# Four edits to a one-core transformer-layer kernel: modulation sums by transposes, chunk states in seven pieces, four output tiles in token halves, last output in four transfers from two queues

## The chip, the cores and the metric

The kernel runs on one core of a Trainium2 chip. A core has a matrix engine (TensorE, PE in the profile; its weight loads are shown apart as PEld), three further compute engines (VectorE or DVE, ScalarE or ACT, GpSimd or POOL), a queue engine that issues transfers (SyncE, SP), and 16 transfer engines (DMA). Each engine runs its own instructions in order and waits on semaphores for the others. Operands lie in an on-chip memory of 128 partitions; TensorE writes its sums into banks of a second memory, from which the other engines read them. The metric is the device time of one execution in microseconds (us); of several runs the median is given.

## What is computed

One layer of a diffusion backbone over 512 latent tokens of width 1024, with 256 context tokens. In outline:

```python
def reference(x, c, ctx, c_ctx, w_mod, b_mod, ...):
    mod = silu(c) @ w_mod + b_mod                       # six vectors of 1024
    sh1, sc1, gt1, sh2, sc2, gt2 = split(mod, 6)
    h_lat = rmsnorm(x, norm1_g) * (1 + sc1) + sh1       # the same for ctx with c_ctx
    p = h @ w_in                                        # z, xs/B/C, dt, q, k, v, gates
    y_ssd = ssd_bidir(...)                              # state-space mixer, 4 groups, both directions
    y_att = window_ctx_attention(...)                   # 16 heads, window of 128, context keys, sink
    o = (g_ssd * (y_ssd @ w_o_ssd) + g_att * (y_att @ w_o_att)) @ w_out
    x = x + gt1 * o
    x = x + gt2 * conv_ffn(rmsnorm(x, norm2_g) * (1 + sc2) + sh2, w_up, ..., w_down)
    return rmsnorm(x, final_g)
```

`ssd_bidir` cuts the 512 tokens into four chunks of 128. For each chunk a state (decayed sum of B times the scaled inputs) is carried on from the chunk before; the states of the backward direction go the other way round. The first states come from the context tokens.

## The kernel before

Activations are held with channels on the partitions and tokens along the free axis, 512 columns (`L`). Every fp32 product is split into a high and a low part: for a weight block of 128x128, TensorE does three matmuls, high weight by high input (line 192), high by low (line 193), low by high (line 195). A `gemm` makes an output tile of 128 channels over eight such blocks, so it has 24 matmuls of 512 columns for the latent tokens (`LAT`) or of 256 for the context (`CTX`).

**Weights.** A tile's weights arrive by `load_raw` as 512 KB in one of three raw buffers (`wraw`), issued on SyncE's queue. ScalarE makes the high part (line 149), VectorE the low part (line 150), each into one of two buffers, and then the raw buffer is free again. `run` walks a list of steps and loads the weights of the next step ahead of the one that runs. The 32 blocks of the modulation weights (`wm`, `msteps`) go through the same raw buffers, without a split. `weave(a, b)` puts the steps of b evenly between those of a.

**Modulation sums (`m_step`).** The four vectors that are needed late (gt1, sh2, sc2, gt2; 32 columns of 128 in `mod2`) come from 32 blocks, four blocks to a group of four columns, so eight groups. VectorE multiplies each block by the conditioning vector and adds up over the blocks in one tile `tm` (lines 550 and 552). With a group's last block, TensorE sums over the partitions by four fp32 matmuls of the tile's four 128-column pieces by a column of ones (line 556), each done in two passes, and VectorE adds the bias to the 128x4 result (line 558).

**Projection and chunk states.** For each of four groups, six projection steps follow each other (B, C, four tiles of xs). Each ends with a convolution over tokens and a silu (lines 860 to 869, the last being `tc` at line 869). The result must be transposed to tokens on the partitions: it is put on a list `TURN`, and `turn()` (lines 883 to 890) does the transposes of all that is on the list, four of 128x128 for the latent tokens and two for the context (line 888). After the four xs tiles, `states()` puts six pieces on a list `BETWEEN`; `gemm` takes one piece after every block k with k % 3 == 1, that is three in a gemm of eight blocks. The pieces are `first` (the outstanding transposes, then VectorE weighs the context's inputs for the backward direction, `xw`, line 947), `second` (TensorE sums the context, line 978, and VectorE weighs for the forward direction), `third` (the same sum for the forward direction, and the first latent chunk is weighed), and three times `back` (TensorE sums a chunk, line 960; GpSimd decays the state before, line 962; VectorE adds, line 963; the next chunk is weighed). The gemms they go into are those of the next group's B step (`b_fn`: one for the latent, one for the context tokens), and for the last group those of steps that fill in (branch gates and z).

**Output tiles.** After the merge of the branches, `out_step(o)` makes tiles 0 to 4 of the product with `w_out` over all 512 tokens: gemm, VectorE adds to x (line 1238), ScalarE squares (line 1187) and VectorE adds up the squares. These five are woven with six modulation blocks (numbers 18 to 23): one each after tiles 0 to 3, two after tile 4. Blocks 16 to 19 make a group, and so do 20 to 23. Tiles 5 to 7 are in `out_last`: token half by token half, three tiles a half, 24 matmuls of 256 columns each (lines 1196 to 1198), written down in TensorE's order by hand. Their weights go to buffers of their own (`wlast`, in space that the SSD output held before), loaded and split like the rest. In the second half's gemms stand the steps of the second norm for the first half: `half_sums`, `root`, `spread`.

**Tail (`down_last`, `finish`).** The last tile of the down projection is made in token halves, and with each half the final norm is done: squares, sums, root (on GpSimd, line 245), spread over the partitions by transposes, then eight chunks of 128x256 are scaled (VectorE line 1383; for the second half GpSimd does two of them, chunks 5 and 6, line 1381, from copies that ScalarE has scaled before) and sent out by five transfers, all on SyncE's queue (line 1385): chunks (0, 1), (2, 3), (4), (5, 6), (7).

The order of instructions on each engine is found by a scheduler from estimates, except where the program writes it out (`manual_schedule`); a list of instructions in the built program shows what order it chose. In that order the changed program differs from the one before around the output tiles, as told under the change.

## Time and profile before

| what | value |
|---|---|
| median of 3 runs | 1293.3 us (1292.84 to 1293.32) |
| profiled execution | 1291.25 us |
| span of the profile | 1289.5 us |
| mean granted TensorE clock | 0.998 |
| ScalarE busy | 664.8 us (52%) |
| GpSimd busy | 138.6 us (11%) |
| moved by transfers | 168.66 MB, mean 131 GB/s |

The profile is of one execution. The span goes from its first instruction to its last; the device time is some 2 us more. The chain of waits follows back from the last instruction to what released it, so a share of it is a share of the time that can be saved at all. A group's line reads: source line, engine, operation, tile written from tiles read, shape, count, then busy us and mean ns of one, and last the idle time of the engine just ahead of them with what ended it. A row of the timeline has start, duration, engine, line, operation, and in square brackets the idle time ahead of it. Matmuls are pipelined, so a matmul's own 390 ns is not what it adds; the distance from one start to the next is.

### The profile page before, as it was taken

The numbers are of one execution on the slowest core, as the hardware profiler recorded it, in microseconds if no ns is written. First come the engines' busy times: TensorE is split into PE (matmuls) and PEld (weight loads), VectorE is DVE, ScalarE is ACT, GpSimd is POOL, SyncE is SP. The second block draws the span as 40 slices with busy tenths as digits, with TensorE's granted clock in tenths as the row PEclk, the third lists the DMA queues.
The fourth block names the chain that finished last, engine by engine and source line by source line (L and its number), as shares of the span: only waits on it lengthen the run. The fifth ranks groups of instructions, "written<-read, shape, count | busy, mean of one in ns | idle before, by whom it ended". The sixth has DMA issues, their size and how long they took to land.

```text
span 1289.5 us, 17298 instructions
## 1 busy us (share of the span) xinstructions
PE 1260.1 (98%) x6482; PEld 1025.6 (80%) x6482; DVE 899.2 (70%) x1431; ACT 664.8 (52%) x1230; POOL 138.6 (11%) x113
## 2 busy tenths in 40 slices
PE   7999999999999999999999999999999999999997
PEld 4698777887778878788787777888888888888886
DVE  3867888778495588888888757776677767772323
ACT  3568888767434466475673744223544444442221
POOL 0000000000000043433434440000200000000000
PEclk9999999999999999999999999999999999999999
DMA  8621112222345245454445558867133433333331
GB/s 321 255 94 51 42 58 66 66 74 66 99 127 184 82 117 137 139 134 131 137 140 170 165 192 290 252 221 229 33 115 115 131 114 114 115 107 93 92 101 66
DMA packets 86931, 168.66 MB, mean 131 GB/s; under 512 B 6784, under 2 KB 42112, under 8 KB 86848
## 3 DMA queue, kind: packets, MB, share of 16 engines
q1 hardware_dynamic: 86848, 167.56, 41.5%
q8 instruction: 51, 0.84, 0.3%
q14 instruction: 32, 0.26, 0.1%
HBM read 150.62 MB, written 16.91 MB: 130 GB/s over the span
## 4 chain that ended last, share of the span: by engine, by line
PE 84%; DVE 7%; ACT 5%; issue 2%; DMA 1%; POOL 0%; SPq 0%; DVEq 0%; ACTq 0%; POOLq 0%
PE acc L193 21%; PE acc L192 21%; PE acc L195 21%; PE mis L1054 2%; PE mis L1047 2%; PE score L668 2%; PE pt L697 2%; PE mis L404 2%; PE mis L960 1%; PE po L702 1%; DVE wlo L150 1%; PE mis L888 1%; PE mis L978 1%; PE po L703 1%; PE acc L1196 1%
## 5 line engine op out<-in xcount | busy, mean ns | idle before, releaser
L150 DVE TENSOR_TENSOR wlo<-wraw,whi 128x1024 fp32r<-128x1024 f32 x161 | 203.8, 1266 | 133.0 <-ACT whi L149 131.7
L149 ACT CAST whi<-wraw 128x1024 fp32r<-128x1024 f32 x161 | 166.7, 1036 | 220.7 <-PE acc L193 186.6
L192 PE MATMUL acc<-hlh,whi 128*128 128x512 f32 (+1 forms) x496 | 204.1, 412 | 0.1
L193 PE MATMUL acc<-hll,whi 128*128 128x512 f32 (+1 forms) x496 | 196.1, 395 | 0.0
L195 PE MATMUL acc<-hlh,wlo 128*128 128x512 f32 (+1 forms) x496 | 195.4, 394 | 0.2 <-DVE wlo L150 0.2
L192 PE MATMUL acc<-mh,whi 128*128 128x512 f32 x376 | 146.5, 390 | 0.0
L193 PE MATMUL acc<-ml,whi 128*128 128x512 f32 x376 | 146.4, 389 | 0.0
L195 PE MATMUL acc<-mh,wlo 128*128 128x512 f32 x376 | 146.3, 389 | 0.0
L192 PEld LDWEIGHTS acc<-hlh,whi 128*128 128x128 f32 (+1 forms) x496 | 93.0, 187 | 21.3 <-issue 4.1
L193 PEld LDWEIGHTS acc<-hll,whi 128*128 128x128 f32 (+1 forms) x496 | 93.0, 187 | 19.9 <-issue 4.1
L195 PEld LDWEIGHTS acc<-hlh,wlo 128*128 128x128 f32 (+1 forms) x496 | 92.8, 187 | 19.5 <-issue 1.0
L195 PEld LDWEIGHTS acc<-mh,wlo 128*128 128x128 f32 x376 | 70.6, 188 | 14.8
L192 PEld LDWEIGHTS acc<-mh,whi 128*128 128x128 f32 x376 | 70.6, 188 | 14.7
L193 PEld LDWEIGHTS acc<-ml,whi 128*128 128x128 f32 x376 | 70.6, 188 | 14.6 <-DVE ml L1165 0.2
L962 POOL TENSOR_TENSOR st<-st,eT 128x512 f32<-128x512 f32 x24 | 32.8, 1368 | 410.3 <-ACT st L980 396.7
L860 ACT ACTIVATE ta<-acc,half 128x512 f32<-128x512 f32 (+1 forms) x66 | 46.6, 706 | 41.0 <-PE acc L195 41.0
L245 POOL TENSOR_TENSOR rs<-ms,phalf 128x2 f32<-128x2 f32 (+1 forms) x7 | 6.1, 877 | 548.9 <-DVE ms L244 548.9
L675 DVE CUSTOM_DVE_ANT_0 p<-score,winm,nsink 128x512 f32<-128x512 f32 (+1 forms) x64 | 52.0, 812 | 15.0 <-PE score L668 14.2
L192 PE MATMUL acc<-fh,whi 128*128 128x512 f32 x154 | 60.0, 390 | 0.0
L195 PE MATMUL acc<-fh,wlo 128*128 128x512 f32 x154 | 59.9, 389 | 0.0
L193 PE MATMUL acc<-fl,whi 128*128 128x512 f32 x154 | 59.9, 389 | 0.0
L679 ACT ACTIVATE p<-p,mneg 128x512 f32<-128x512 f32 (+1 forms) x64 | 49.7, 777 | 17.2 <-DVE mneg L675 16.9
(320 smaller groups left out, 2818.8 us busy)
## 6 DMA issues: line engine op xcount, KB each, us to landing
wraw<-wup SPq DMA_DIRECT2D x44, 512.0 KB, 3.6
fb<-cs_d SPq DMA_DIRECT2D x32, 512.0 KB, 6.7
wraw<-wm SPq DMA_DIRECT2D x32, 512.0 KB, 3.6
wraw<-wx SPq DMA_DIRECT2D x24, 512.0 KB, 3.6
wm<-wm SPq DMA_DIRECT2D x16, 512.0 KB, 8.1
wraw<-wz SPq DMA_DIRECT2D x16, 512.0 KB, 3.6
wraw<-wos SPq DMA_DIRECT2D x16, 512.0 KB, 4.6
wraw<-wdn SPq DMA_DIRECT2D x16, 512.0 KB, 3.5
```

Of the source, the lines that this page charges most:

```text
L149: S.copy(hi[:, :n], r[:, :n])
L150: V.tensor_tensor(lo[:, :n], r[:, :n], raw(hi[:, :n]), ALU.subtract)
L192: T.matmul(ps, wh, xh[:, k0 + k, :], start=a, stop=False)
L193: T.matmul(ps, wh, xl[:, k0 + k, :], start=False, stop=False)
L195: T.matmul(ps, wl, xh[:, k0 + k, :], start=False, stop=b)
L404: T.matmul(pg[i], w[a][:, i * P : (i + 1) * P], h[b], start=st and a + b == 0, stop=en and a == 1, skip_group_check=True,)
L668: T.matmul(ps[:, o : o + w], Q[h][:, b * P : (b + 1) * P], k[:, j, z[0] * P : z[0] * P + w], start=v == 0 and o % 512 in (0, P), stop=v == ...
L675: V.tensor_tensor_reduce(p[:, :n], ps[:, o0 : o0 + n], m, op0=ALU.add, op1=ALU.min, scale=1.0, scalar=nsink[:, h : h + 1], accum_out=mn,)
L679: S.activation(p[:, :n], p[:, :n], AF.Exp, bias=mn, scale=-1.0, accum_out=den[:, i : i + 1])
L697: T.transpose(pt[:, i * P : (i + 1) * P], pts[i][:, c * P : (c + 1) * P], ident)
L860: S.activation(o[:, :n], ps[:, :n], AF.Identity, scale=hcol(base_w, stride + i), bias=hcol(base_b, i))
L962: G.tensor_tensor(h8(n), h8(s), bc64(eT[:, z0 : z0 + 8, c]), ALU.mult)
```

## The change

- The four matmuls by ones become four transposes into one bank, and VectorE sums each 128-column piece with one reduction and adds the bias in a second small instruction.
- `turn(n)` does the first n transposes on the list and leaves the rest. A piece that does only the first entry (the latent tokens' four transposes) stands ahead of `first`, which makes seven pieces; the last `back` then falls into the gemm after.
- Output tile 4 moves from `out_step` to `out_last`, which now has four tiles in two halves. The six modulation blocks are woven with four tiles: one after tile 0, two after tile 1, one after tile 2, two after tile 3. On SyncE's queue the loads before ran: tile 0, m18, tile 1, m19, tile 2, m20, tile 3, m21, tile 4, m22, m23, tiles 5 to 7. They now run: tile 0, m18, tile 1, m19, m20, tile 2, m21, tile 3, m22, m23, tiles 4 to 7. On VectorE the first product of m20 stands ahead of the split of tile 3, its second one behind it.
- The output of each half goes in four transfers of two chunks, alternately from SyncE's and ScalarE's queue; the chunks that GpSimd scales are 4 and 5.

```diff
--- before.py
+++ after.py
@@ -553,9 +553,10 @@
             if kk == 3:
                 ps = misb()
                 for c in range(4):
-                    T.matmul(ps[:, c : c + 1], acc[:, c * P : (c + 1) * P], ones[:, 0:1], start=True, stop=True)
+                    T.transpose(ps[:, c * P : (c + 1) * P], acc[:, c * P : (c + 1) * P], ident)
                 z = slice(4 * cg, 4 * cg + 4)
-                V.tensor_tensor(mod2[:, z], ps[:, 0:4], vec[:, V_BMOD + 16 + 4 * cg : V_BMOD + 20 + 4 * cg], ALU.add)
+                V.tensor_reduce(mod2[:, z], ps.rearrange("p (c q) -> p c q", c=4), axis=AX.X, op=ALU.add)
+                V.tensor_tensor(mod2[:, z], mod2[:, z], vec[:, V_BMOD + 16 + 4 * cg : V_BMOD + 20 + 4 * cg], ALU.add)
 
         return [("m", i)], fn
 
@@ -880,14 +881,14 @@
     GR = [{} for _ in range(4)]
     TURN = []
 
-    def turn():
-
-        for t, n, put in TURN:
+    def turn(n=None):
+
+        for t, n_, put in TURN[:n]:
             ps = misb()
-            for c in range(n):
+            for c in range(n_):
                 T.transpose(ps[:, c * P : (c + 1) * P], t[:, c * P : (c + 1) * P], ident)
             put(ps)
-        TURN.clear()
+        del TURN[:n]
 
     def proj_steps(g):
         d = GR[g]
@@ -986,6 +987,9 @@
             def first():
                 turn()
                 weigh_ctx(1)
+
+
+            BETWEEN.append(lambda: turn(1))
 
             def second():
                 sum_ctx(1)
@@ -1223,8 +1227,8 @@
         return fn
 
 
-    for o in (5, 6, 7):
-        ELSEWHERE["out", o] = piece_in("yh%d" % (o - 5))
+    for o in (4, 5, 6, 7):
+        ELSEWHERE["out", o] = piece_in("yh%d" % (o - 4))
 
     def out_step(o):
         def fn(w):
@@ -1241,8 +1245,8 @@
         return [("out", o)], fn
 
     def out_last(*w):
-        xt = [cp.tile([P, L], F32, tag="ld", name="ld", bufs=3) for _ in range(3)]
-        for i, o in enumerate((5, 6, 7)):
+        xt = [ldt[0]] + [cp.tile([P, L], F32, tag="ld", name="ld", bufs=3) for _ in range(3)]
+        for i, o in enumerate((4, 5, 6, 7)):
             nc.sync.dma_start(xt[i], xT[o // 2, :, (o % 2) * L : (o % 2 + 1) * L])
         pf = F["pf"] = misb()
         F["r2"] = []
@@ -1255,17 +1259,17 @@
 
         with tc.manual_schedule(engines={mybir.EngineType.PE}):
             for u, z in enumerate(HALF):
-                for i in range(3):
+                for i in range(4):
                     after = {}
                     if u == 1:
                         after = {0: {5: root}, 1: {4: spread}}.get(i, {})
-                    if i == 2:
+                    if i == 3:
                         after[2] = lambda u=u: half_sums(pf, q2, u)
                     ps = accb()
                     half_gemm(ps, mh, ml, z, w[i], 8, 0, 8, after)
-                    x = x1[1][:, 1 + i, z]
-                    V.scalar_tensor_tensor(x, ps[:, :HL], g1h[:, 5 + i : 6 + i], xt[i][:, z], ALU.mult, ALU.add)
-                    if i == 0:
+                    x = x1[1][:, i, z]
+                    V.scalar_tensor_tensor(x, ps[:, :HL], g1h[:, 4 + i : 5 + i], xt[i][:, z], ALU.mult, ALU.add)
+                    if i < 2:
                         sq = half_squares([x])[0]
                         V.tensor_tensor(q2[:, z], q2[:, z], sq, ALU.add)
                 F["sq2"] = half_squares([x1[1][:, 2 + i, z] for i in range(2)])
@@ -1374,7 +1378,7 @@
             if u:
                 r3s = tmp("tc")[:, :HL]
                 S.copy(r3s, rms_spread(r["s"], 2)[:, :HL])
-            for cs in ((0, 1), (2, 3), (4,), (5, 6), (7,)):
+            for i, cs in enumerate(((0, 1), (2, 3), (4, 5), (6, 7))):
                 for c in cs:
                     x = x1[c // 4][:, c % 4, z]
                     if u and c in scaled:
@@ -1382,7 +1386,7 @@
                     else:
                         V.scalar_tensor_tensor(x, x, col(V_FG, c), r3[:, :HL], ALU.mult, ALU.mult)
                 n, c = len(cs), cs[0]
-                nc.sync.dma_start(
+                (S if i % 2 else nc.sync).dma_start(
                     out[c * P : (c + n) * P, z].rearrange("(a p) t -> p a t", a=n), x1[c // 4][:, c % 4 : c % 4 + n, z]
                 )
                 if c == 2:
@@ -1400,7 +1404,7 @@
             V.scalar_tensor_tensor(xo, ps[u][:, :HL], mod2[:, 31:32], xo, ALU.mult, ALU.add)
             r["sq"] = half_squares([xo])
 
-        for i, c in enumerate((5, 6)):
+        for i, c in enumerate((4, 5)):
             scaled[c] = tmp("te")[:, :HL]
             S.activation(scaled[c], x1[1][:, c % 4, HALF[1]], AF.Copy, scale=col(V_FG, c))
         ps = [accb(), accb()]
@@ -1420,9 +1424,9 @@
         + fill[n3:]
         + [os_step(o) for o in range(2)]
         + weave([os_step(o) for o in range(2, 8)], msteps[8:18])
-        + weave([out_step(o) for o in range(5)], msteps[18:24])
+        + weave([out_step(o) for o in range(4)], msteps[18:24])
         + [([], vectors)]
-        + [([("out", o) for o in (5, 6, 7)], out_last), ([], close_c1)]
+        + [([("out", o) for o in (4, 5, 6, 7)], out_last), ([], close_c1)]
         + weave([up_step(t) for t in range(NFF)], msteps[24:])
         + [down_step(o) for o in range(7)]
         + [([("dn", 21 + i) for i in range(3)], down_last)]
```

## The prediction

> **What bounds the kernel now.** First the page's busy line and the shares of the chain that ended last.
>
> ```profile
> span 1289.5 us, 17298 instructions
> ...
> PE 1260.1 (98%) x6482; PEld 1025.6 (80%) x6482; DVE 899.2 (70%) x1431; ACT 664.8 (52%) x1230; POOL 138.6 (11%) x113
> ...
> PE 84%; DVE 7%; ACT 5%; issue 2%; DMA 1%; POOL 0%; SPq 0%; DVEq 0%; ACTq 0%; POOLq 0%
> ```
>
> TensorE is busy for 98% of the span, and 84% of the chain lies on it, so an edit pays if it takes instructions out of TensorE's stream, or shortens one of the few places where that stream waits. VectorE and ScalarE count where they are late with something TensorE wants, and in the tail, where TensorE has nothing left. So I went by stage: the chain of waits for each edited line, TensorE's own rows around the state pieces, the transfer queue's rows around the output tiles, the tail. The profiled execution took 1291.25 us with a span of 1289.5; the median shown is 1293.3, so 2 us of the forecast is only the step from that execution to the median.
>
> **A, modulation sums.** Chain of waits, first and last of the eight groups of sums, and a row of sixteen transposes:
>
> ```profile
> 522.80 1.75 PE mis L1076 x16
> ...
> 579.01 0.79 PE mis L556 x8
> ...
> 1155.75 0.79 PE mis L556 x8
> ```
>
> Groups of instructions:
>
> ```profile
> L963 DVE TENSOR_TENSOR st<-st,mis 128x512 f32<-128x512 f32 x24 | 16.3, 680 | 2.0 <-PE mis L960 2.0
> L556 PE MATMUL mis<-ones,tm 128*128 128x1 f32 x64 | 7.6, 239 | 0.0
> ```
>
> The 64 matmuls are eight groups of four columns, two passes each: 0.79 us a group on the chain. Four transposes instead cost 4 × 1.75/16 = 0.44 by the first row. The saving is 0.35 a group by these rows; where a dense matmul follows, I read about 0.1 more lost after the old group (a weight load per single-column pass), so 0.35 to 0.47, eight times: −2.8 to −3.8, and I take **−3.5 us**. VectorE gets a reduction of 128x512 from PSUM and a 128x4 add where it had one such add. No reduction stands in the trace. The nearest row reads 512 columns from PSUM and takes 0.68 us, the two-operand form, and I take 0.7; eight make 5.6 us on an engine that is idle 30% of the span. I cost that at nothing: it is hidden while TensorE runs the next gemm, whose low weights were split one step ahead. With that cover gone it costs 0.7 a group (last rival). The bank of sums is read some 0.7 us longer; four others remain.
>
> **B, chunk states in seven pieces.** TensorE's rows at the second and third group's first piece, then one row of the longest waits (total, times, longest):
>
> ```profile
> 610.80 0.39 PE L192 MATMUL acc<-hlh,whi 128*128 128x512 f32 x1
> 611.97 0.41 PE L888 MATMUL mis<-ident,tc 128*128 128x128 f32 x2 [0.78 <-DVE tc L869]
> ...
> 695.07 0.41 PE L888 MATMUL mis<-ident,tc 128*128 128x128 f32 x2 [0.78 <-DVE tc L869]
> ...
> 698.67 0.70 PE L978 MATMUL mis<-xw,Bkc 128*128 128x512 f32 x1 [0.23 <-DVE xw L947]
> ```
>
> ```profile
> PEld mis L978 <- DVE xw L947: 4.2, 8, 0.9
> ```
>
> A gemm's matmuls start 0.23 apart, so between 610.80 and 611.97 TensorE lost 1.17 − 0.23 = 0.94 us waiting for the context columns' convolved tile; the same, with the same idle entry, ahead of 695.07. The weight loads of the context sums then waited 4.2 us in all for the weighted tile, in part beside a matmul still running; the one case with a number on TensorE itself is the 0.23 of 698.67, against a longest wait of 0.9. I count half of the 4.2 as TensorE's, so all stalls here are 1.9 + 2.1 = 4 us. The change puts the four transposes of the main columns into a piece of their own, and the two of the context columns one piece later, so nine matmuls of the gemm stand between where seven stood. Two more of 0.227 hide 0.45 of each 0.94; the waits for the weighted tile may go or stay, and I take half of their 2.1. That is −0.9 and −1.1: **−2 us**, from 0 to −4. Nothing is added. What moves: the last piece of the backward states now goes into the next gemm, so in the last group its VectorE work, one weighted tile, stands later, just ahead of the chunks' first use; a loss there would be up to that tile's product, 0.7 by the row of 680 ns, and the bound of 0 covers it only with a gain elsewhere.
>
> **C, output tile 4 in halves.** First the price on TensorE, from the chain at the border:
>
> ```profile
> 890.32 0.23 PE acc L195
> 890.55 0.79 PE mis L556 x8
> ...
> 891.56 0.12 PE acc L1197
> ```
>
> A tile was 24 matmuls at 0.227; in halves it is 48 at 0.120: **+0.3 us**. The larger effect is in the order of loads. With four tiles woven with six modulation steps, two steps now follow output tile 1, so the step's second block is loaded ahead of tile 2's weights. There are three raw buffers, and each load is issued when the next buffer comes free, as issues and releases show (before). SyncE's queue, then VectorE, the list of issues (median us to landing) and ScalarE:
>
> ```profile
> 861.55 0.33 SPq L145 DMA_DIRECT2D wraw<-wout  x1
> 866.44 0.33 SPq L145 DMA_DIRECT2D wraw<-wm  x1
> 867.71 0.33 SPq L145 DMA_DIRECT2D wraw<-wout  x1
> ...
> 869.99 0.33 SPq L145 DMA_DIRECT2D wraw<-wm  x1
> ...
> 875.46 0.33 SPq L145 DMA_DIRECT2D wraw<-wout  x1
> 877.24 1.90 SPq L145 DMA_DIRECT2D wraw<-wm  x2
> ...
> 881.86 3.95 SPq L145 DMA_DIRECT2D wraw<-wout  x3
> ```
>
> ```profile
> 863.93 0.75 DVE L552 SCALAR_TENSOR_TENSOR tm<-wraw,csil,tm 128x512 f32<-128x512 f32 x1 [0.90 <-DMA wraw<-wm]
> ...
> 865.20 1.22 DVE L150 TENSOR_TENSOR wlo<-wraw,whi 128x1024 fp32r<-128x1024 f32 x1
> ...
> 868.73 1.23 DVE L150 TENSOR_TENSOR wlo<-wraw,whi 128x1024 fp32r<-128x1024 f32 x1
> ...
> 874.10 0.17 DVE L558 TENSOR_TENSOR mod<-mis,vec 128x4 f32<-128x4 f32 x1
> 874.21 1.23 DVE L150 TENSOR_TENSOR wlo<-wraw,whi 128x1024 fp32r<-128x1024 f32 x1
> ...
> 876.47 2.32 DVE L552 SCALAR_TENSOR_TENSOR tm<-wraw,csil,tm 128x512 f32<-128x512 f32 x3
> 879.71 0.75 DVE L1238 SCALAR_TENSOR_TENSOR x<-acc,g1h,te 128x512 f32<-128x512 f32 x1 [0.92 <-PE acc L195]
> 880.61 1.23 DVE L150 TENSOR_TENSOR wlo<-wraw,whi 128x1024 fp32r<-128x1024 f32 x1 [0.15 <-ACT whi L149]
> ```
>
> ```profile
> wraw<-wm SPq DMA_DIRECT2D x32, 512.0 KB, 3.6
> ```
>
> ```profile
> 886.43 1.05 ACT L149 CAST wlast<-wraw 128x1024 fp32r<-128x1024 f32 x1 [5.30 <-DMA wraw<-wout]
> 888.24 1.05 ACT L149 CAST wlast<-wraw 128x1024 fp32r<-128x1024 f32 x1 [0.23 <-DMA wraw<-wout]
> ```
>
> The issues of 866.44 and 869.99 come with the ends of the splits of 865.20 and 868.73. A load issued at 881.86 had landed at 886.43: 4.57 us with others in flight, and 1.05 for the cast and 1.23 for the low part follow. Now the changed order. Its slot at 861.55 goes to the modulation block; tile 2's weights go when tile 1's are split, 865.0 (the product of 863.93 no longer ahead of the split) to 866.4, and are split by 871 to 873. Tile 3's load goes then, and its low part ends by 877 to 879.5; TensorE wants it at 879.2 (tile 2 ended shortly ahead of 879.71; the shorter sums take off 0.35). The last two modulation blocks and tile 4's weights wait in turn for that split, for the block held since 861.55 (its second product stands behind the split on VectorE, 0.7 + 0.75) and for the next one (two products, 1.5): tile 4's load goes at 880 to 882.5, lands 4.6 later at 884.6 to 887, and its low part is ready at 887 to 889.5. TensorE has finished tile 3 at 879.2 + 24 × 0.227 = 884.6, the four transposes at 885.1, and wants that low part at 885.3: a new stall of 1.5 to 4.5 us, 0 if all lands as early as 3.6 us (the usual figure of a raw load in the list of issues). I take **+2.7 us**. Before, this margin was there: the same weights were split in step at 880.6. Behind the late split on VectorE stand only those of tiles 5 to 7, at 1.83 us of landing distance against 2.9 us of matmuls per half tile, so the stall comes once. The tail of the last output half and the norm after it are unchanged in place.
>
> **D, last output.** SyncE's issues by line, VectorE's and GpSimd's last work, and us, DMA share and GB/s in the last stretches:
>
> ```profile
> L1385 SPq DMA_DIRECT2D out<-x x10: 345/395/466, 1278.8 to 1286.6; - x10
> ```
>
> ```profile
> 1282.98 2.44 DVE L1383 SCALAR_TENSOR_TENSOR x<-x,vec,mis 128x256 f32<-128x256 f32 x6 [1.37 <-PE mis L251]
> ```
>
> ```profile
> 1283.70 1.41 POOL L1381 TENSOR_TENSOR x<-te,tc 128x256 f32<-128x256 f32 x2 [1.25 <-ACT tc L1376]
> ```
>
> ```profile
> 1286.00:1287.00 1.00, 0.00 (x0) 0.00 (x0) 0.00 (x0) 0.00 (x0) 0.00 (x0) 0.50 1.02 358
> 1287.00:1288.00 1.00, 0.00 (x0) 0.00 (x0) 0.00 (x0) 0.00 (x0) 0.00 (x0) 0.50 1.09 381
> 1288.00:1289.00 1.00, 0.00 (x0) 0.00 (x0) 0.00 (x0) 0.00 (x0) 0.00 (x0) 0.50 0.14 47
> ```
>
> VectorE ends at 1285.42, the last of the issues starts at 1286.6: 1.2 us go into issuing one after another. But from 1286 to 1288 the transfer engines are full, so only an earlier start of the stream helps. Chunks 2 and 3 are done four sixths into the 2.44, at 1284.6, and ScalarE can issue them then, where SyncE got to what followed its first transfer only at about 1285.1, waiting for GpSimd: **−0.4 us**, from −0.8 to +0.2 (an issue on ScalarE has no row; SyncE's is 0.395, and one of them now stands ahead of ScalarE's square of the other half).
>
> The Trainium skill ("DMA: Bandwidth & Descriptors", section "Issuing engines are not separate DMA queues") says that transfers started from several engines run on the same sixteen transfer engines and interleave, and that only issue time is saved, usually little beside the transfer. The share of 1.02 and 1.09 agrees; by that rule the second queue by itself is worth at most two issues, 0.8, and with full engines nothing, which would make the sum 0.4 smaller.
>
> **Sum.** −3.5 − 2.0 + 0.3 + 2.7 − 0.4 = −2.9 us: 1288.3 on the profiled execution's 1291.25, and **1290.4** on the median of 1293.3.
>
> **Rivals.** *No new stall at the output tiles.* If the raw loads land in 3.6 us as most do, tile 4's low part is there in time and the sum is −5.6: 1287.7. For it: that median. Against it: the load of 881.86 took 4.57.
>
> *The seven pieces do nothing.* If TensorE's waits there are set by VectorE's and ScalarE's chain alone, the idle time moves from one piece to the next: B is 0 and the sum −0.9, 1292.4. For it: both 0.94 gaps end with the same VectorE tile. Against it: two more matmuls do stand ahead of the wait.
>
> *Slower: the reduction is not covered.* VectorE runs in order; the reduction waits for TensorE's transposes, and the next low weights stand behind it. If each of the eight makes TensorE wait for its length, 8 × 0.7 = 5.6, and the sum is +2.7: 1296.0. It decides from 2.9 us on (no gain left), and from 5.5 on the kernel is measurably slower. For it: at 874.10 and 874.21 a split follows the sums at once. Against it: 30% of VectorE is idle, and the splits are a step ahead.
>
> **How the numbers follow.** Forecast 0.42, no stall 0.22, pieces without effect 0.16, slower 0.20. A measurement of this kernel can tell 0.2%, 2.6 us, from no change. The forecast lies at that bound (−2.9), with its own range of 1288.5 to 1292: a little over half of it counts as faster (0.23 of 0.42). Faster 0.23 + 0.22 = 0.45; same 0.19 + 0.16 = 0.35; slower 0.20. Downwards the range goes a little past the no-stall case by B's and D's lower ends, 1286.5; upwards to the slower case, 1296.0.
>
> **What would show it.** A: the groups at that line read 0.44 on the chain, not 0.79, and no row of the dense gemms after them waits for low weights. B: the two idle entries of 0.78 ahead of the context transposes fall to some 0.3. C: TensorE's row of the first half tile has an idle entry of 1.5 to 4.5 us ended by the split of tile 4's weights; none there means the first rival. D: the last transfer is issued by 1285.6 and the span ends within 4 us of VectorE's last row. Wrong altogether: the eight reductions in front of waits of TensorE, or a reduction well over 1 us.

## The result

| | median | runs | lowest to highest |
|---|---|---|---|
| before | 1292.84 us | 7 | 1291.53 to 1293.32 |
| changed | 1298.76 us | 7 | 1294.51 to 1302.62 |

The ratio is 1.0042, with a 95% interval of 1.0024 to 1.0060: the changed kernel is slower by 5.4 us by the ratio and 5.9 by the medians, where 2.9 us faster was forecast. The changed kernel's times also spread over 8 us, those of before over 2, and by and large the longer a run, the lower its mean granted clock: 1294.51 us at 0.996, 1302.62 at 0.990. The profile of after is of the shortest of the seven, so it shows only part of the loss.

Its page, span, busy line and the shares of the chain:

```profile
span 1292.7 us, 17284 instructions
...
PE 1259.2 (97%) x6474; PEld 1025.4 (79%) x6474; DVE 902.7 (70%) x1441; ACT 664.5 (51%) x1231; POOL 134.9 (10%) x113
...
PE 75%; DVE 12%; ACT 6%; DMA 4%; issue 2%; POOL 1%; SPq 0%; DVEq 0%; ACTq 0%; POOLq 0%
```

TensorE's work is 0.9 us less, but its share of the chain went from 84% to 75%, and VectorE's from 7% to 12%: TensorE waits where it did not. To find where, I took the same matmuls in both traces (the first or last of a kind) and subtracted their start times, counted from the span's start:

| stretch, by TensorE's rows | before, us | changed, difference |
|---|---|---|
| first attention projection to the last transposes of the context's columns | 338.2 to 695.2 | +1.5 |
| from there to the first product of the SSD output | 695.2 to 768.9 | +1.3 |
| to the first norm's spread | 768.9 to 794.3 | +1.4 |
| to the first output tile | 794.3 to 862.1 | −0.5 |
| output tiles | 862.1 to 910.5 | +1.8 |
| up projection | 910.5 to 1156.4 | −0.9 |
| down projection | 1156.4 to 1278.7 | 0.0 |
| from its last product to the end | 1278.7 to 1289.5 | 0.0 |

Ahead of 338 us the two profiles differ by −1.3, in a stage that the change does not touch. The sums over the modulation columns save 0.44 in each of eight groups, two of them in the first two rows of the table, so the chunk states cost some 3.7 us there (an estimate: 1.5 + 1.3 + 0.9).

**A.** Groups of instructions of after:

```profile
L558 DVE TENSOR_REDUCE mod<-mis 128x4 f32<-128x512 f32 x8 | 5.5, 684 | 1.8 <-PE mis L556 1.8
L556 PE MATMUL mis<-ident,tm 128*128 128x128 f32 x32 | 4.8, 273 | 0.4 <-DVE tm L552 0.4
```

32 transposes took the place of 64 passes, and the reduction takes 0.684 us.

**B.** TensorE's rows at the forward sum of the context, second and third group, and at the last group's chunk products; then VectorE's and GpSimd's rows ahead of the first of them:

```profile
535.09 1.12 PE L979 MATMUL mis<-xw,Bkc 128*128 128x512 f32 x2 [1.05 <-DVE xw L948]
...
611.48 0.41 PE L889 MATMUL mis<-ident,tc 128*128 128x128 f32 x2 [0.34 <-DVE tc L870]
619.31 1.13 PE L979 MATMUL mis<-xw,Bkc 128*128 128x512 f32 x2 [1.06 <-DVE xw L948]
...
728.24 1.10 PE L1058 MATMUL mis<-xs,E 128*128 128x64 f32 x8 [0.58 <-DVE E L1042]
730.27 1.10 PE L1058 MATMUL mis<-xs,E 128*128 128x64 f32 x8 [0.92 <-DVE E L1042]
```

```profile
528.23 3.11 DVE L948 TENSOR_TENSOR xw<-xsc,TC 128x512 f32<-128x512 f32 x3
531.68 1.88 DVE L150 TENSOR_TENSOR wlo<-wraw,whi 128x1024 fp32r<-128x1024 f32 x1 [0.34 <-DMA zs<-zs_d]
533.49 1.54 DVE L948 TENSOR_TENSOR xw<-xsc,TC 128x512 f32<-128x512 f32 x1
```

```profile
532.70 1.78 POOL L963 TENSOR_TENSOR st<-st,eT 128x512 f32<-128x512 f32 x1 [0.21 <-ACT st L981]
```

The idle entry ahead of the context's transposes fell from 0.78 to 0.34 as worked out (611.48). But the pieces come later against VectorE's own work, and VectorE's order is no longer the one of before: a weight split now stands between the third and the fourth weighing of the context (before, all four stood ahead of it), and the sum that needs the fourth waits 1.05. The split and the weighing are also longer than usual, 1.88 and 1.54 us, while GpSimd's product of 532.70 runs. The prediction's rows at 611.97 and 695.07, called the second and third group's, are the third and the last group's: the entry of 0.78 at the later place falls to 0.34 with the extra piece in the last group only, and stays with it in the first three.

**The clock.** Stretches of 2 us with TensorE's busy time, and near the end of the row the granted clock; first the changed kernel at the first products of the SSD output, then the kernel before there:

```profile
772.00:774.00 2.00, 1.58 (x12) 1.39 (x10) 1.06 (x3) 0.72 (x1) 0.35 (x1) 1.00 0.84 293
774.00:776.00 2.00, 1.52 (x4) 0.49 (x3) 1.17 (x2) 1.40 (x2) 0.66 (x1) 1.00 0.87 277
776.00:778.00 2.00, 1.84 (x5) 1.43 (x6) 1.91 (x4) 1.88 (x4) 0.00 (x0) 0.66 0.92 330
778.00:780.00 2.00, 2.00 (x6) 1.54 (x5) 1.66 (x3) 0.75 (x2) 0.00 (x0) 0.50 0.96 302
```

```profile
774.00:776.00 2.00, 2.00 (x10) 1.41 (x9) 1.42 (x4) 1.34 (x3) 0.00 (x0) 1.00 1.00 354
776.00:778.00 2.00, 1.72 (x7) 1.15 (x7) 2.00 (x3) 1.93 (x3) 0.00 (x0) 1.00 0.91 301
778.00:780.00 2.00, 1.91 (x9) 1.24 (x8) 1.65 (x3) 2.00 (x4) 0.00 (x0) 1.00 1.03 265
```

Just after TensorE has waited for the split SSD output (idle entries of 0.42, 0.28 and 0.29 from 773.78 to 776.16) the clock stands at half for about 3.4 us, during which 2 us hold 6 matmuls instead of 10: about 1.7 us lost. That is the +1.4 of the table's third row. But it doesn't take the change to bring it about. The run with the edit to the output alone (below) has the kernel of before up to the tail, and its profile shows the same at the same place:

```profile
774.00:776.00 2.00, 1.71 (x5) 0.98 (x6) 1.75 (x3) 1.83 (x3) 0.56 (x1) 0.78 1.02 364
776.00:778.00 2.00, 2.00 (x6) 1.55 (x6) 1.78 (x4) 1.69 (x4) 0.00 (x0) 0.50 0.83 290
```

The kernel before waits there too (0.66, 0.29 and 0.28); that its profile has no stretch at half clock ahead of the tail is luck of that execution. A stretch that costs 1.7 us lowers a run's mean clock by 0.0013 (half of 3.4 in 1293), so 0.001 of mean clock stands for some 1.3 us; by this estimate the clock accounts for nearly all of the 8 us between the shortest and the longest run of the changed kernel.

**C.** TensorE's waits at the border from whole tiles to halves:

```profile
887.34 0.63 PE L556 MATMUL mis<-ident,tm 128*128 128x128 f32 x4 [0.36 <-DVE tm L552]
888.40 0.39 PE L1200 MATMUL acc<-mh,wlast 128*128 128x256 f32 x1 [0.44 <-ACT wlast L149]
889.66 0.39 PE L1202 MATMUL acc<-mh,wlast 128*128 128x256 f32 x1 [0.76 <-DVE wlast L150]
```

TensorE waits for VectorE's product of the last modulation block first, then for the cast and the split of tile 4's weights: 1.6 us of idle entries, and 2.3 us on the stretch, which is +1.8 with 0.9 saved by two groups of sums and 0.3 paid for the halves.

**D.** The output's issues from both queues:

```profile
L1389 SPq DMA_DIRECT2D out<-x x4: 373/384/395, 1282.1 to 1288.8; - x4
L1389 ACTq DMA_DIRECT2D out<-x x4: 379/386/430, 1282.9 to 1288.9; - x4
```

The last issue now starts with the end of VectorE's work (1286.48 + 2.44 = 1288.92 in this trace) instead of 1.2 us after it, and the span ends 3.8 us after that work instead of 4.1. But the tail as a whole is as long as before.

### The profile page after: what moved, and what is told of

Read it like the earlier page. It is cut to its first block, busy times and chain, and to the rows that moved or that the text cites. A ratio compares the mean times of both kernels' runs of the same rounds, so it can differ in the third digit from the quotient of the medians.

```text
span 1292.7 us, 17284 instructions
## 1 busy us (share of the span) xinstructions
PE 1259.2 (97%) x6474; PEld 1025.4 (79%) x6474; DVE 902.7 (70%) x1441; ACT 664.5 (51%) x1231; POOL 134.9 (10%) x113
## 3 DMA queue, kind: packets, MB, share of 16 engines
q10 hardware_dynamic: 1088, 1.05, 0.2%
## 4 chain that ended last, share of the span: by engine, by line
PE 75%; DVE 12%; ACT 6%; DMA 4%; issue 2%; POOL 1%; SPq 0%; DVEq 0%; ACTq 0%; POOLq 0%
PE acc L193 18%; PE acc L192 18%; PE acc L195 18%; DVE wlo L150 3%; PE score L669 2%; PE pt L698 2%; PE mis L1058 2%; PE mis L404 2%; PE mis L1051 2%; PE mis L961 1%; DMA wraw<-wout 1%; PE po L703 1%; ACT whi L149 1%; PE acc L1200 1%; PE acc L1202 1%
## 5 line engine op out<-in xcount | busy, mean ns | idle before, releaser
L150 DVE TENSOR_TENSOR wlo<-wraw,whi 128x1024 fp32r<-128x1024 f32 (+1 forms) x160 | 202.9, 1268 | 136.6 <-ACT whi L149 135.1
L149 ACT CAST whi<-wraw 128x1024 fp32r<-128x1024 f32 (+1 forms) x160 | 165.5, 1035 | 213.9 <-PE acc L193 165.8
L192 PE MATMUL acc<-mh,whi 128*128 128x512 f32 x368 | 143.5, 390 | 0.0
L195 PE MATMUL acc<-mh,wlo 128*128 128x512 f32 x368 | 143.3, 389 | 0.0
L193 PE MATMUL acc<-ml,whi 128*128 128x512 f32 x368 | 143.3, 389 | 0.0
```

The costliest lines, as they stand in the source:

```text
L149: S.copy(hi[:, :n], r[:, :n])
L150: V.tensor_tensor(lo[:, :n], r[:, :n], raw(hi[:, :n]), ALU.subtract)
L192: T.matmul(ps, wh, xh[:, k0 + k, :], start=a, stop=False)
L193: T.matmul(ps, wh, xl[:, k0 + k, :], start=False, stop=False)
L195: T.matmul(ps, wl, xh[:, k0 + k, :], start=False, stop=b)
```

## The experiments

Each kernel ran in turn with the kernel before on the same chip; the first four ran together, and so did the next four and the next three. "Before" is the median of the kernel before in the same session.

| run | median, us | before | ratio | 95% interval |
|---|---|---|---|---|
| sums alone | 1292.02 | 1293.44 | 0.9985 | 0.9974 to 0.9995 |
| pieces alone | 1298.55 | 1293.44 | 1.0042 | 1.0028 to 1.0056 |
| tiles alone | 1293.29 | 1293.44 | 1.0001 | 0.9992 to 1.0010 |
| output alone | 1292.26 | 1293.44 | 0.9994 | 0.9985 to 1.0003 |
| all but the pieces | 1293.90 | 1292.76 | 1.0010 | 1.0002 to 1.0019 |
| pieces, last group only | 1297.23 | 1292.76 | 1.0036 | 1.0023 to 1.0048 |
| pieces, first three groups | 1295.34 | 1292.76 | 1.0018 | 1.0009 to 1.0026 |
| all but the pieces, filled | 1297.75 | 1292.76 | 1.0036 | 1.0024 to 1.0047 |
| pieces, weighed early | 1295.71 | 1293.45 | 1.0022 | 1.0012 to 1.0031 |
| sums and output | 1292.43 | 1293.45 | 0.9990 | 0.9978 to 1.0002 |
| all but the pieces, blocks earlier | 1293.23 | 1293.45 | 1.0000 | 0.9992 to 1.0009 |
| sums and output, squares later | 1288.75 | 1294.27 | 0.9953 | 0.9936 to 0.9969 |

### One part at a time

The first four kernels take one part of the diff each, the rest as before.

The sums alone: 

> The modulation sums by transposes alone, all else as before. Theory (the pieces and the output tiles lose the time): the sums save 0.35 to 0.47 us a group, so about 3 us: 1289 to 1290.5 where the kernel before has 1292.8; the chain shows the groups' TensorE work at 0.44. Rival (the reductions on VectorE lose the time): no gain or slower, 1293 to 1299, with weight loads of TensorE waiting for splits behind the reductions. Granted clock: 0.998 as before by the theory that stalls at other places pull it down; 0.990 to 0.996 if the transposes themselves do.

The pieces alone: 

> The seven pieces alone. Theory: VectorE's new order puts a weight split between the third and fourth weighing of the context, so TensorE waits about 1 us in the second and third group and again at the last group's first chunk: about +3.5 us, 1296, more in runs with a lower granted clock. Rival (the pieces gain as predicted, the loss is elsewhere): −2, 1291.

The tiles alone: 

> Four output tiles in token halves alone, with the modulation blocks spread over four tiles. Theory: the stall at tile 4's weights, worked out at 2.7 and seen as about 2.3 us between the output tiles' start and the up projection: 1295 to 1296. Rival (that loss comes only with the reductions on VectorE): within 0.5 of the kernel before.

The output alone: 

> The last output in four transfers from two queues alone. Theory: within 0.4 us of the kernel before, as the changed kernel's tail from the last product to the end is as long as before. Rival (two queues slow each other): +0.5 or more. The granted clock stays at 0.998 by both.

The pieces alone lose all of it: 1.0042, the ratio of the whole change, and 1298.55 us where I expected 1296. The sums gain, but 1.4 us at the median and not 3. The tiles alone cost nothing, a miss of my expectation of 2 to 3 us. The output is within its interval of no change.

In the trace of the pieces alone, the waits at the last group's second chunk are those of the changed kernel (0.58 and 0.92), and there the clock falls behind them. Its stretches of 2 us:

```profile
730.00:732.00 2.00, 1.11 (x9) 0.97 (x8) 1.30 (x3) 1.77 (x6) 0.00 (x0) 1.00 0.21 64
732.00:734.00 2.00, 1.39 (x9) 1.39 (x10) 2.00 (x3) 2.00 (x5) 0.00 (x0) 0.85 0.59 158
734.00:736.00 2.00, 2.00 (x5) 0.97 (x5) 1.10 (x3) 1.76 (x7) 0.96 (x1) 0.50 0.74 207
736.00:738.00 2.00, 2.00 (x9) 1.59 (x9) 0.99 (x4) 1.05 (x4) 1.92 (x3) 0.79 0.59 225
```

In the changed kernel's profile the same two waits are there without that. So the clock can fall behind these waits and need not. That the waits of the pieces make it fall more often is argued, not shown: the mean clocks of these five runs are 0.991 to 0.996, those of before in the session 0.995 on average.

### Which pieces

```diff
-            BETWEEN.append(lambda: turn(1))
+            if g == 3:
+                BETWEEN.append(lambda: turn(1))
```

> The extra piece in the last group only, else the kernel before. Theory (both places lose): the first chunk's waits of 0.6 and 0.9 and, in most runs, 1.7 of halved clock behind them: +2 to +3, so 1295.5 to 1296.5. Rival (the loss is all in the second and third group, where a split stands ahead of the fourth weighing): 1293 to 1294.

And the other way round, `if g < 3`:

> The extra piece in the first three groups only. Theory: TensorE waits 0.8 to 1.05 for the fourth weighing where it waited some 0.3 before, and the 0.94 waits ahead of the context's transposes shrink to 0.4 or less: +1 to +2.5, so 1294.5 to 1296. Rival (all in the last group): 1292.5 to 1293.5.

Both lose: 4.5 us in the last group, 2.6 in the first three, together 7.1 and so more than the 5.1 of all four. Neither rival holds. The excess goes with the clock: the four runs with the last group alone have a mean clock of 0.993 against 0.996 for those of before in the session, some 3 us. In the traces, with the stretches at half clock taken off (1.7 us each), the stage from the first attention projection to the first product of the SSD output is longer than before by 1.8 us with the last group alone and 2.0 with the first three, and by 4.1 with all four. In the trace with the last group alone the stretch from the last context transposes to the first product of the SSD output is 3.2 us longer than before, with the clock at half once; in the one with the first three groups the idle entries of 1.05 stand where they stood in the changed kernel.

### The order on VectorE

```diff
-        def weigh(x, c, w):
-            xw = bp.tile([P, 512], F32, tag="xw", name="xw", bufs=2)
+        def weigh(x, c, w, xw=None):
+            xw = xw or bp.tile([P, 512], F32, tag="xw", name="xw", bufs=2)
...
             def first():
                 turn()
                 weigh_ctx(1)
+                weigh_ctx(0)
 
             def second():
                 sum_ctx(1)
-                weigh_ctx(0)
```

(the forward weighings go to `tmp("te")`, under a name of their own)

> The extra piece in the first three groups, as in the run of that name, but the two forward weighings of the context go into two spare tiles in the same piece as the backward ones, so that all four stand ahead of the weight split on VectorE. Theory (the split ahead of the fourth weighing is what loses there): the idle entries of 0.8 to 1.05 at the forward sum in the second and third group go, and the loss of 2.6 with them: 1292 to 1293.5. Rival (the transposes' new place loses the time itself): 1295 as before.

The time did not follow the theory. The entries of 1.05 went, as expected, but the loss stayed (1295.71 against 1295.34, each some 2.4 above its own before). TensorE's rows show waits in other places, the first in the second group, the other in the last:

```profile
553.72 1.10 PE L1051 MATMUL mis<-st,CT 128*128 128x512 f32 x2 [0.72 <-DVE E L1040]
...
731.40 1.10 PE L1058 MATMUL mis<-xs,E 128*128 128x64 f32 x8 [0.90 <-DVE E L1042]
```

With the weighings ahead of the split, the split and what follows it are later, and the group's first chunk waits behind its decay tile E. But the edit also weighs early in the last group, which has no extra piece here, and the row at 731.40 is that group's. By the traces, none with a stretch at half clock before the tail, the first three groups lose 0.9 us here (up to the last context transposes) where they lost 2.0, and the last group loses 1.1 where it lost nothing. So the split's place was about half of the loss in the first three groups, and the early weighings cost as much in the last one: the run's time hides that. What is left, and what all the kernels with the seven pieces have in common, is that the chain of VectorE's, GpSimd's and ScalarE's work at a group's end begins one piece later, while its end is wanted at the same place; that this alone makes the rest of the loss is argued.

### The tiles and the sums together

All but the pieces:

> The whole change without the seven pieces. Theory (the pieces alone cost the time): the three other edits measured 1292.0, 1293.3 and 1292.3 alone against 1293.4, sum −2.7, so about 1290.7 and faster than the kernel before. Rival (the edits add up to a loss when together): 1293.5 or more.

The expectation failed: three parts that alone gave −1.4, −0.2 and −1.2 give +1.1 together. The waits at the border, in its trace:

```profile
886.53 0.63 PE L556 MATMUL mis<-ident,tm 128*128 128x128 f32 x4 [1.94 <-DVE tm L552]
888.35 0.39 PE L1199 MATMUL acc<-mh,wlast 128*128 128x256 f32 x1 [0.75 <-DVE wlast L150]
```

With the tiles alone there is no idle entry there. VectorE's rows tell why: first the tiles alone, then with the sums by transposes.

```profile
875.42 0.49 DVE L550 TENSOR_SCALAR tm<-wraw,csil 128x512 f32<-128x512 f32 x1
875.94 0.75 DVE L552 SCALAR_TENSOR_TENSOR tm<-wraw,csil,tm 128x512 f32<-128x512 f32 x1
...
878.16 1.23 DVE L150 TENSOR_TENSOR wlo<-wraw,whi 128x1024 fp32r<-128x1024 f32 x1 [0.87 <-ACT whi L149]
```

```profile
874.52 0.48 DVE L550 TENSOR_SCALAR tm<-wraw,csil 128x512 f32<-128x512 f32 x1
...
877.66 1.22 DVE L150 TENSOR_TENSOR wlo<-wraw,whi 128x1024 fp32r<-128x1024 f32 x1 [2.59 <-ACT whi L149]
...
879.40 2.32 DVE L552 SCALAR_TENSOR_TENSOR tm<-wraw,csil,tm 128x512 f32<-128x512 f32 x3
```

Alone, both products of modulation block m20 stand ahead of tile 3's split, its raw buffer is free at 876.7, and the next block is issued then. With the sums' edit in VectorE's order, the second product stands behind the split, and the next block goes out at 878.9. TensorE is also there about a microsecond sooner. The 2.7 us of the forecast is this wait, and it needs both parts.

The blocks earlier:

```diff
-        + weave([os_step(o) for o in range(2, 8)], msteps[8:18])
-        + weave([out_step(o) for o in range(4)], msteps[18:24])
+        + weave([os_step(o) for o in range(2, 8)], msteps[8:20])
+        + weave([out_step(o) for o in range(4)], msteps[20:24])
```

> The whole change without the seven pieces, with modulation blocks 18 and 19 moved to the branch merge ahead, so that one block follows each of output tiles 0 to 3 and none is loaded ahead of tile 2's weights. Theory (the order of loads makes the wait at tile 4): no idle entry over 0.5 there, the stretch from the first output tile to the up projection 3 us shorter than without this, 1290.5 to 1292. Rival (the wait is the transfer rate's, whatever the order): 1293.5 to 1294, with the same idle entries.

The waits at tile 4 are gone, and the stretch from the first output tile to the up projection is 3.0 us shorter than without this, as the theory had it. Yet the time is 1293.23, no better than before: the branch merge ahead became 4.5 us longer. Three of the waits there:

```profile
818.67 0.50 PE L195 MATMUL acc<-yh,wlo 128*128 128x512 f32 x1 [0.53 <-DVE wlo L150]
842.00 0.50 PE L195 MATMUL acc<-yh,wlo 128*128 128x512 f32 x1 [0.53 <-DVE wlo L150]
...
860.15 0.50 PE L195 MATMUL acc<-yh,wlo 128*128 128x512 f32 x1 [0.97 <-DVE wlo L150]
```

So the order of loads does make the wait at tile 4, but from the branch merge to the tiles the raw loads have no room: blocks that leave one step make another late. In the time the rival was nearer than the theory.

### Filling the wait

```diff
             ps = accb()
+            if o == 0:
+                fp = misb()
+                for i in range(4):
+                    T.matmul(fp, w0[0][:, :P], w0[0][:, :L], start=True, stop=True)
```

> The whole change without the seven pieces, and four matmuls of 512 columns into a bank that nobody reads, ahead of the first product of the SSD output. Theory (the waits there, 1.3 us in all, let TensorE's clock go to half for some 3.3 us in most runs, which costs 1.7): no halved clock at 770 to 785, 1 to 2 us faster than the same without them, about 1289, and fewer runs with a low mean clock. Rival (the clock falls for another reason): the same as without them, or up to 0.9 slower.

It took 1297.75 us, 3.9 more than without them, so neither forecast holds, and it did not answer its question. The four matmuls ran ahead of the wait instead of in it, the norm's eight small matmuls that had stood ahead of the wait now stood behind it, and the wait became one of 1.77 us. Behind it the clock stood at half for 6.8 us, and again for 6.8 at 889.5 to 896.3, behind a wait of 2.27 us at tile 4. In this trace longer waits are followed by longer stretches at half clock; it doesn't say that a filled wait brings none.

### What the sums lost

The sums and the output together:

> The sums by transposes and the output in four transfers, tiles and pieces as before. Theory (the tiles' edit is what gives the gain of these two back when all three are together, by its wait at tile 4): 1290 to 1291.5. Rival (the gains of the two do not add up): 1292.5 or more.

1292.43, between the two forecasts, and an interval that holds no change: part of the 3.5 is still missing. TensorE's row in this trace, VectorE's rows ahead, and the last of these on both engines in the kernel before:

```profile
900.74 0.58 PE L234 MATMUL mis<-rmsc,q 128*128 128x1 f32 x4 [1.19 <-DVE q L1271]
```

```profile
896.01 0.68 DVE L558 TENSOR_REDUCE mod<-mis 128x4 f32<-128x512 f32 x1
896.72 1.23 DVE L150 TENSOR_TENSOR wlo<-wraw,whi 128x1024 fp32r<-128x1024 f32 x1
897.86 0.68 DVE L1189 TENSOR_TENSOR q<-q,tc 128x512 f32<-128x512 f32 x1
...
900.18 0.42 DVE L1271 TENSOR_TENSOR q<-q,tc 128x256 f32<-128x256 f32 x1
```

```profile
897.41 0.42 DVE L1270 TENSOR_TENSOR q<-q,tc 128x256 f32<-128x256 f32 x1
```

```profile
898.12 0.50 PE L234 MATMUL mis<-rmsc,q 128*128 128x1 f32 x4
```

TensorE waits 1.19 us for the sum of squares that `half_sums` reads, where it waited for nothing before. The reduction after tile 4 stands ahead of that sum, but it isn't what makes the wait. Counted from the first matmul of the output tiles (864.44 here, 862.14 before), TensorE gets to the halves 1.0 us sooner, as two groups of sums are shorter, and VectorE's sum ends 0.5 us later (36.2 against 35.7). From its addition for tile 4 to that sum VectorE takes 5.2 us here with the reduction, and 5.5 before without it, where it stood idle for 0.8 in between. The addition itself comes 0.8 later, behind the split of the last output tile's weights, whose cast waits for the load. The kernels with the pieces in the last group or in the first three, whose sums are those of before, also wait at this row, 0.31 and 0.67. So most of the wait is the saving itself: TensorE is sooner at a place where VectorE, behind the weight loads, is not. So, last, the reading of the squares four blocks later:

```diff
                     if i == 2:
-                        after[2] = lambda u=u: half_sums(pf, q2, u)
+                        after[6] = lambda u=u: half_sums(pf, q2, u)
```

> The sums by transposes and the output in four transfers, and the sums of squares of the first token half (half_sums) four blocks later in TensorE's order, after block 6 of the third half tile instead of block 2. Theory (the 1.1 to 1.2 us of idle ahead of those sums comes from VectorE's reduction and the two steps behind it, and is what the saving of the transposes lost): no idle entry over 0.2 there, 1 us faster than without this, about 1291.3 and faster than the kernel before by 0.15% or more. Rival (the wait moves on to the next step, the roots or the second norm): no change against the run without it, 1292.4.

The row has no idle entry any more:

```profile
900.91 0.50 PE L234 MATMUL mis<-rmsc,q 128*128 128x1 f32 x4
```

1288.75 us, a ratio of 0.9953 (0.9936 to 0.9969): faster than both kernels. The stretch over the output tiles is 1.2 us shorter in this trace than without the move; the rest of the 3.7 us between the two medians goes with the mean clocks (0.994 to 0.998 here, 0.990 to 0.997 without the move). From the first attention projection to the end its trace is 3.2 us shorter than that of before; the medians differ by more, 5.5, as the runs of before in that session had lower mean clocks (0.991 to 0.997, against 0.994 to 0.998).

## Why the prediction was wrong

**What bounds the kernel.** This was right: the losses are places where TensorE waits or, behind such waits, runs at half clock, and the gain is what was taken out of its stream.

**A, right in its size, wrong in what it is worth.** The saving on TensorE was put at 0.35 to 0.47 a group, and the stretch with two groups is 0.9 shorter. The reduction was taken as 0.7 and takes 0.684. "I cost that at nothing" held for the reduction's own length, as far as the traces show; with the tiles' edit it failed by the order that the reduction leaves on VectorE (C). What was also wrong is that every group's saving was counted as time: at the second norm's first sums TensorE, sooner by two groups' saving, waits 1.1 to 1.2 us for squares that come no sooner. The rival in which the reduction isn't covered has eight waits of TensorE, each of the reduction's length; no trace here shows those.

**B, the step that failed.** "**−2 us**, from 0 to −4", and "Nothing is added". It measured +5.1 alone, of which some 4.1 stand as waits in the stage of the chunk states in its trace. The narrow working was right, the idle entry ahead of the context's transposes did shrink, from 0.78 to 0.34. But two things were left out. The pieces after the new one start later and their results are wanted at the same place: a weight split got ahead of the fourth weighing, and TensorE waited 1.05 at the forward sums; where that order was mended, 0.7 of waiting turned up at the group's first chunk. And the last group's later chain, which I bounded by 0.7 and set against "a gain elsewhere", made two waits of 0.58 and 0.92 at the second chunk. The bound of 0 was no bound: moving a piece later can be a loss where VectorE's chain is the slower one, and the prediction's own row, eight weight loads of these sums waiting 4.2 us for VectorE's weighed tile, said that it was.

Neither did I have the clock among the costs. The forecast treated a wait of TensorE as costing its own length. In the traces of the pieces alone and of the last group alone, a stretch at half clock behind the last group's waits cost 1.7 us more.

**C, right only together with A.** The chain of loads was worked out for the changed kernel and held for it (1.5 to 4.5, 2.7 taken; 2.3 in the changed kernel and, counted in the same way, 3.8 without the pieces). Alone there is no such wait: VectorE takes the second product ahead of the split, so the very order on which the working rested comes with the sums' edit.

**D.** −0.4 was forecast, and the interval of the part alone, −1.9 to +0.4 us, holds both that and no change. In the two profiles the tail is equally long, 10.8 us from the last product to the end: the 0.3 us saved behind VectorE's last row is given back ahead of it, where the six scalings start 0.25 us later after the last product. Why they do stays open. Over all fourteen traces the tail takes 10.5 to 10.8 us in the seven kernels with this edit and 10.8 to 11.3 in the seven without, on average 0.3 less, close to the forecast; the medians can't tell so little. The Trainium skill ("DMA: Bandwidth & Descriptors", section "Issuing engines are not separate DMA queues") has it that issue time is all that a second queue saves; by that rule nothing more was to be had, and the trace agrees.

**The sum.** By the medians, the parts alone (−1.4, +5.1, −0.2 and −1.2) make +2.3; A, C and D together came out 3.9 above the sum of theirs (+1.1 against −2.8), which makes +6.2, and the whole change measured +5.9. A, C and D were forecast at −0.9 together and measured +1.1, 2.0 off; B was forecast at −2 and measured +5.1, 7.1 off and with the wrong sign. B is the error that made the forecast wrong.

## What to carry to other kernels

When a step is moved later to hide a wait, follow the chain behind it to the place where its last result is wanted, and count how much of that chain's engine is left between: if the waits of today end on that engine, later can be a loss. Count a saving on the bounding engine only up to the next place where it waits for one that has become no faster. Cost an extra instruction by the order in which it leaves the others on its engine, not by the engine's idle share. And test parts in pairs: two that cost nothing alone can cost microseconds where one changes the order on which the other rests.

## What the runs showed of the hardware

**TensorE's clock can go to half behind short waits.** Idle entries of 0.42, 0.28 and 0.29 within 3 us (changed kernel), of 0.69 and 0.29 (output alone), or of 0.58 and 0.92 (pieces alone) were followed by half clock for about 3.4 us in some executions and not in others: 0.66, 0.29 and 0.28 in the kernel before, whose instructions up to the tail are those of the output alone, and 0.58 and 0.92 in the changed kernel were not. The Trainium skill ("TensorE: Matmul & The Clock Gate", section "What's actually happening") says that the clock is halved after an idle window of about 3.4 us, that the window runs freely, and that the count of slow matmuls at a kernel's start varies from run to run with it. The length of the halved stretches and the spread agree; that the window must be idle does not: TensorE was busy for about three quarters of the 4 us ahead (1.58 and 1.52 of each 2 us at 772 to 776 in the changed kernel).

**VectorE is slowed by GpSimd.** The same 128x512 weighing took 0.72 us in the kernel before and 1.56 in the kernel with the pieces alone, where GpSimd's product started with it. Kernel before, then the pieces alone, VectorE and GpSimd:

```profile
723.45 0.72 DVE L947 TENSOR_TENSOR xw<-xs,TA 128x512 f32<-128x512 f32 x1
```

```profile
726.80 1.56 DVE L947 TENSOR_TENSOR xw<-xs,TA 128x512 f32<-128x512 f32 x1
```

```profile
726.76 1.06 POOL L962 TENSOR_TENSOR st<-st,eT 128x512 f32<-128x512 f32 x1 [1.40 <-DVE st L963]
```

The difference is 0.84 us, most of GpSimd's 1.06. The Trainium skill ("SBUF — State Buffer", section "Who interferes with whom") says that a VectorE instruction with two inputs in SBUF contends with a GpSimd instruction that reads SBUF, and that the later one waits; the rows agree.

The changed kernel has the same meeting at the last group's second chunk, where TensorE's products by the states start at the same time in both profiles (725.79 before, 725.78 changed). VectorE's first step of the decay tile that TensorE then waits for, in the kernel before, and the rows that lead to it in the changed kernel:

```profile
724.23 0.73 DVE L1036 COPY_PREDICATED E<-sel,mis 128x512 f32<-128x512 uint8 x1
```

```profile
723.65 0.68 DVE L964 TENSOR_TENSOR st<-st,mis 128x512 f32<-128x512 f32 x1
...
724.46 1.56 DVE L948 TENSOR_TENSOR xw<-xs,TA 128x512 f32<-128x512 f32 x1
...
726.08 0.72 DVE L1040 COPY_PREDICATED E<-sel,mis 128x512 f32<-128x512 uint8 x1
```

The step is 1.85 us later: 0.84 by the longer weighing, 0.6 by the state's addition, which the extra piece has put ahead of it, and 0.4 by what came before. So at this place nearly half of the delay is the meeting. How much it makes of the pieces' loss elsewhere was not tried.
